# Left-operand sums of a seven-product output projection: accumulating transfers in the place of VectorE's additions

## The chip, the core and the metric

One NeuronCore of a Trainium2 chip runs the whole program in one launch. The metric is device time in microseconds (us), as the median over executions; a profile of one execution stands beside it.

## What is computed

One layer of an encoder block over 1024 tokens of width 1024: a feed-forward half step, a mixer (neighbourhood attention and a state-space branch, merged by gates), a second feed-forward half step, an embedding of the input, a norm. The change lies in the mixer's merge and its output projection:

```
g_attn, g_ssm = jnp.split(jax.nn.sigmoid(gates), N_BRANCH, axis=-1)
h = h + (g_attn * y_attn + g_ssm * y_ssm) @ w_out[i]
h = h + 0.5 * swiglu(rms_norm(h, ffn2_norm[i]), ...)
```

All arithmetic is float32. A product is made of three matmuls: each operand is split into a rounded part (hi, by a ScalarE copy into the reduced type, line 151) and the rest (lo, by a VectorE subtraction, line 152), and hi x hi, hi x lo and lo x hi are summed (`mm3`, lines 182 to 184).

## The kernel before, in words

Activations lie transposed, channels on the 128 partitions, tokens along the free dimension in two halves t = 0, 1 of 512. A tile is 128 x 512 float32, 256 KB.

The merge makes sixteen tiles `mg[m, t]` (m = 0 to 7 are the channel blocks): `branches` multiplies the two mixer outputs by their weights, `gated` (lines 1501 and 1502) multiplies by the gates and adds.

The output projection is a product of 2 x 2 blocks by seven block products instead of eight (`A7` gives their left operands: a12, a11, s1, s2, s4, s3, a22). For each block index j = 0 to 3 the left operand's four blocks are a = mg[j, 0], b = mg[4+j, 0], c = mg[j, 1], d = mg[4+j, 1]. The seven left operands are b, a, the first sum s1 = c + d, the second sum s2 = s1 - a, the third sum s4 = b - s2, the difference s3 = a - c, and d. `out_left` returns the operand of product i and the additions that follow its split: line 1519 makes s1 (`ss`) behind product 1, lines 1522 and 1523 make s2 and s3 behind product 2, line 1526 makes s4 behind product 3. All sixteen (four lines, four j) run on VectorE.

The right operands, blocks of the weight w_out, need sums too. They are made by `taken_from` (lines 406 and 407): ScalarE turns the sign of the block and a transfer issued from GpSimd (`G.dma_start` with `accum_op=add`) adds the other block from HBM onto it.

There are 28 steps (i, j), product i outermost. `out_prep` (split of the left operand, right operand by `b_operand`, then the additions) runs four steps (LA) ahead of `out_run`, which issues twelve matmuls onto four banks. The products go to banks dz, dx, dy (ACC7 = Z X Y X Y X X); at j = 3 line 1548 adds the four banks onto the residual h on VectorE, and for i = 1, 4, 5, 6 `merged` adds the squares for the next norm (ScalarE line 221 or 224, VectorE line 225) and stores h. At step 20 the next norm's statistic for t = 0 is started: a matmul by a matrix of ones over the summed squares (line 241), then lines 203 to 206, and the scaling of h by line 372 with its splits.

TensorE's instructions keep the order in which they are written. Those of the other engines and the GpSimd transfers are put in order by a planner at build time, which simulates the engines and goes by priority; line 1548 and `gated` have a raised priority. On the chip each engine's queue then runs in that fixed order, and each instruction waits for its own operands and buffers. Buffers that matter: `w` (20 tiles, the weight splits; the next stage takes twelve of them from step 4 on), `tmp` (17 tiles, the left splits ah and al, gates, squares), `hid` (the pool of 56 tiles with mg, ss and the weight blocks).

Of the kernel before, what the change touches and what calls it, by code (L numbers as in the profile page):

```python
# [8 lines left out]
F32 = mybir.dt.float32  # L9
F32R = mybir.dt.float32r  # L10
I32 = mybir.dt.int32
AF = mybir.ActivationFunctionType
ALU = mybir.AluOpType
# [25 lines left out]
def encoder_block(ctx, tc, I, out):  # L39
    nc = tc.nc  # L40
    V, A, G, T = nc.vector, nc.scalar, nc.gpsimd, nc.tensor
# [26 lines left out]
    def at(kind, shape, dt, name):  # L68
        pool, tag, bufs = cur[kind]
        return pool.tile(list(shape), dt, tag=tag, bufs=bufs, name=name)  # L70
# [7 lines left out]
    def thid(name, shape=(P, HT), dt=F32R):  # L78
        return at("hid", shape, dt, name)

    def tmp(name, shape=(P, HT), dt=F32):
        return at("tmp", shape, dt, name)
# [67 lines left out]
    def split(hi, lo, src, eng=V):  # L150
        A.copy(hi, src)  # L151
        return eng.tensor_tensor(lo, src, hi.bitcast(F32), ALU.subtract)  # L152
# [16 lines left out]
    def loadh(src, st_kind="tmp", w_kind="w", eng=V):  # L169

        res = []
        for i in range(2):
            st = at(st_kind, [P, HT], F32, "wsh")
            nc.sync.dma_start(st, src[:, i * HT:(i + 1) * HT])
            hi, lo = at(w_kind, [P, HT], F32R, "whh"), at(w_kind, [P, HT], F32R, "whl")
            split(hi, lo, st, eng)
            res += [(hi[:, ksl(k)], lo[:, ksl(k)]) for k in range(4)]
        return res
# [230 lines left out]
    def b_operand(blk, i, src=None):  # L409


        b11, b12, b21, b22 = blk
        if src is None and i in (2, 3, 6):
            V.tensor_tensor(b11, (b12, b22, None, None, b21)[i - 2], b11, ALU.subtract)  # L414
        elif src is None and i == 5:
            V.tensor_tensor(b12, b22, b12, ALU.subtract)
        hi, lo = tw("wh", [P, HT]), tw("wl", [P, HT])
        mark["ins"] = split(hi, lo, (b21, b11, b11, b11, b22, b12, b11)[i]).ins
        if src is not None and i in (1, 2, 3):
            taken_from(blk, 0, src[(1, 3, 2)[i - 1]])  # L420
            if i == 2:
                taken_from(blk, 1, src[3])
        return hi, lo
# [1055 lines left out]
    def branches(W, todo):  # L1479

        for i, t, b in todo:
            o = banks[i, t, b] = bank("br")
            for k in range(4):
                mm3(o, W[i][4 * b + k], oy[t][b][k], k == 0, k == 3)
                tick()

    def gates(m, t):
        gts = []
        for b in range(2):
            gt = tmp("gt")  # L1490
            nc.sync.dma_start(gt, g_d[8 * b + m, :, hsl(t)])
            A.activation(gt, gt, AF.Sigmoid)
            gts.append(gt)
        return gts

    def gated(gts, m, i, t):

        mg[m, t] = thid("mg", dt=F32)
        with tc.high_priority(offset=PRI):
            for b, gt in enumerate(gts):  # L1500
                V.tensor_tensor(gt, banks.pop((i, t, b)), gt, ALU.mult)
            V.tensor_tensor(mg[m, t], gts[0], gts[1], ALU.add)

    def out_place(n, j):

        return I["wout"][j + (n // 2) * 4][:, (n % 2) * HT:(n % 2 + 1) * HT]

    def out_load(n):
        for j in range(4):
            blk[j][n] = at("hid", [P, HT], F32, "wblk")  # L1510
            nc.sync.dma_start(blk[j][n], out_place(n, j))

    def out_left(i, j):

        a, b, c, d = (mg.get((m, t)) for t in range(2) for m in (j, 4 + j))

        def s1():
            ss[j] = thid("ss", dt=F32)
            V.tensor_tensor(ss[j], c, d, ALU.add)

        def s2():
            V.tensor_tensor(ss[j], ss[j], a, ALU.subtract)
            V.tensor_tensor(c, a, c, ALU.subtract)

        def s4():
            V.tensor_tensor(b, b, ss[j], ALU.subtract)

        return (b, a, ss.get(j), ss.get(j), b, c, d)[i], {1: s1, 2: s2, 3: s4}.get(i)

    def out_prep(i, j):  # L1530
        src, then = out_left(i, j)
        left = tmp("ah", dt=F32R), tmp("al", dt=F32R)
        split(*left, src)
        made[i, j] = left, b_operand(blk[j], i, [out_place(n, j) for n in range(4)])
        if then is not None:
            then()
# [15 lines left out]
    banks, Wn, mg, ss, made, acc = {}, W0, {}, {}, {}, {}  # L1552
# [3 lines left out]
    for m0 in range(0, NK, 2):  # L1556
        W, Wn = Wn, []
        if m0 == 0:
            Wn = [loadh(I["was"][2 + i]) for i in range(2)]

            branches(W, [(i, t, 0) for t in range(2) for i in range(2)])
        for t in range(2):
            for i in range(2):
                if t == 1 and 0 < m0 < NK - 2:
                    Wn.append(loadh(I["was"][m0 + 2 + i]))
                gts = gates(m0 + i, t)
                branches(W, [(i, t, b) for b in range(m0 == 0, 2)])
                gated(gts, m0 + i, i, t)
            if m0 == NK - 2 and t == 0:
                for s_ in steps[:LA]:  # L1570
                    out_prep(*s_)
        if m0 in (2, 4):
            out_load(2 if m0 == 2 else 0)
    for n in (1, 3):
        out_load(n)
    for n_, (i, j) in enumerate(steps):
        if n_ == 4:
            s7 = Seven(h, 2)
            ffn = Ffn(s7, I["wg2"], I["wu2"], I["wd2"], a2_d, load_h2, done, t0_done2, (8, 11))
            for n in (0, 2, 1, 3):  # L1580
                ffn.load_first(n)
        if n_ == 12:
            for g in range(2):
                ffn.prep(("C", "11", g))
        if n_ == 20:
            start(s7.first(4, 5, 2))
        if n_ + LA < len(steps):
            out_prep(*steps[n_ + LA])
        out_run(i, j)
# [196 lines left out]
def build(nc, shapes):  # L1786
    ins = {k: nc.dram_tensor("in_" + k, s, F32, kind="ExternalInput").ap() for k, s in shapes.items()}
    out = nc.dram_tensor("outT", (1024, SEQ), F32, kind="ExternalOutput").ap()
    with tile.TileContext(nc, schedule_with_timeline_sim=True) as tc:
        with tc.manual_schedule(engines={mybir.EngineType.PE}):  # L1790
            encoder_block(tc, ins, out)
# [12 lines left out]
```

## Time and profile before

| | |
|---|---|
| median of three runs | 2105.99 us (2104.8 to 2106.98) |
| the profiled execution's own time | 2106.49 us |
| its span, first to last instruction | 2104.7 us |
| granted TensorE clock, mean | 0.996 |
| TensorE busy | 2077.2 us (99%) |
| VectorE / ScalarE / GpSimd busy | 1414.2 / 1000.3 / 401.7 us |
| the merge's output projection, steps 0 to 27 | about 1259 to 1346 us of the span |

The page names engines PE (TensorE matmuls), PEld (its weight loads), DVE (VectorE), ACT (ScalarE), POOL (GpSimd), SP (SyncE's queue); a q behind the name is that engine's queue. Times run from the span's start. A line such as L152 is the line of the kernel, and as `split` is a helper, one line stands for splits all over the kernel; the tile names tell them apart (al <- ss is the left operand's split, wl <- wblk the weight's).

### The profile page before, as it was taken

The numbers are of one execution on the slowest core, as the hardware profiler recorded it, in microseconds if no ns is written. First come the engines' busy times: TensorE is split into PE (matmuls) and PEld (weight loads), VectorE is DVE, ScalarE is ACT, GpSimd is POOL, SyncE is SP. The second block draws the span as 40 slices with busy tenths as digits, with TensorE's granted clock in tenths as the row PEclk, the third lists the DMA queues.
The fourth block names the chain that finished last, engine by engine and source line by source line (L and its number), as shares of the span: only waits on it lengthen the run. The fifth ranks groups of instructions, "written<-read, shape, count | busy, mean of one in ns | idle before, by whom it ended". The sixth has DMA issues, their size and how long they took to land.

```text
span 2104.7 us, 28050 instructions
## 1 busy us (share of the span) xinstructions
PE 2077.2 (99%) x9660; PEld 1707.4 (81%) x9660; DVE 1414.2 (67%) x2420; ACT 1000.3 (48%) x1832; POOL 401.7 (19%) x636
## 2 busy tenths in 40 slices
PE   8999999999999999999999999899999999999997
PEld 3788888888888888888888888788888888888886
DVE  7897776667967334777653658896566665786855
ACT  6434333434445333667674635543333334445544
POOL 0047555541000006888100011000000000000000
PEclk9999999999999999999999999999999999999999
DMA  3434444475533552233477754143323338533302
GB/s 133 143 118 154 126 134 126 140 269 165 185 119 107 167 177 68 64 102 97 120 202 263 254 171 91 56 159 111 110 85 126 90 112 296 158 109 92 119 21 81
DMA packets 197455, 285.19 MB, mean 136 GB/s; under 512 B 41536, under 2 KB 80576, under 8 KB 197312
## 3 DMA queue, kind: packets, MB, share of 16 engines
q1 hardware_dynamic: 180160, 258.22, 38.9%
q10 hardware_dynamic: 14848, 20.98, 2.9%
q0 software_dynamic: 2304, 4.20, 1.3%
q8 instruction: 76, 1.25, 0.3%
q14 instruction: 67, 0.55, 0.1%
HBM read 201.01 MB, written 82.31 MB: 135 GB/s over the span
## 4 chain that ended last, share of the span: by engine, by line
PE 93%; DVE 4%; ACT 1%; DMA 1%; issue 1%; SPq 0%; DVEq 0%; ACTq 0%
PE dx L182 4%; PE dx L183 4%; PE dx L184 4%; PE ux L182 3%; PE ux L184 3%; PE ux L183 3%; PE gx L182 3%; PE gx L183 3%; PE gx L184 3%; PE gt L182 3%; PE gt L183 3%; PE gt L184 3%; PE dy L183 2%; PE dy L182 2%; PE dy L184 2%; PE uy L182 2%
## 5 line engine op out<-in xcount | busy, mean ns | idle before, releaser
L151 ACT CAST wh<-hbuf 128x512 fp32r<-128x512 f32 x280 | 172.9, 622 | 392.3 <-PE gx L183 84.0
L152 DVE TENSOR_TENSOR wl<-hbuf,wh 128x512 fp32r<-128x512 f32 x280 | 210.4, 754 | 125.2 <-ACT wh L151 123.0
L151 ACT CAST wh<-wblk 128x512 fp32r<-128x512 f32 x190 | 117.8, 622 | 182.5 <-PE dx L183 78.5
L182 PE MATMUL dx<-ah,wh 128*128 128x512 f32 x416 | 164.0, 394 | 3.9 <-DVE hbuf L1548 3.6
L152 DVE TENSOR_TENSOR wl<-wblk,wh 128x512 fp32r<-128x512 f32 x190 | 130.3, 688 | 53.4 <-ACT wh L151 48.0
L184 PE MATMUL dx<-ah,wl 128*128 128x512 f32 x416 | 162.3, 390 | 0.0
L183 PE MATMUL dx<-al,wh 128*128 128x512 f32 x416 | 162.3, 390 | 0.0
L152 DVE TENSOR_TENSOR al<-araw,ah 128x512 fp32r<-128x512 f32 x154 | 106.0, 692 | 53.7 <-PE dx L183 21.1
L1086 POOL TENSOR_TENSOR sc<-X,rho 128x128 f32<-128x128 f32 x128 | 77.9, 609 | 327.1 <-ACT X L1069 317.1
L182 PE MATMUL gx<-xh,wh 128*128 128x512 f32 x320 | 125.0, 391 | 1.3 <-DVE c L571 1.2
L182 PE MATMUL ux<-xh,wh 128*128 128x512 f32 x320 | 125.1, 391 | 0.3 <-DVE c L571 0.3
L184 PE MATMUL gx<-xh,wl 128*128 128x512 f32 x320 | 124.5, 389 | 0.0
L184 PE MATMUL ux<-xh,wl 128*128 128x512 f32 x320 | 124.5, 389 | 0.0
L183 PE MATMUL ux<-xl,wh 128*128 128x512 f32 x320 | 124.5, 389 | 0.0
L183 PE MATMUL gx<-xl,wh 128*128 128x512 f32 x320 | 124.5, 389 | 0.0
L151 ACT CAST ah<-araw 128x512 fp32r<-128x512 f32 x154 | 95.0, 619 | 47.5 <-PE dx L183 12.7
L182 PE MATMUL gt<-xh,wh 128*128 128x512 f32 x256 | 103.0, 402 | 0.0
L183 PE MATMUL gt<-xl,wh 128*128 128x512 f32 x256 | 99.9, 390 | 0.0
L184 PE MATMUL gt<-xh,wl 128*128 128x512 f32 x256 | 99.8, 390 | 0.0
L182 PEld LDWEIGHTS dx<-ah,wh 128*128 128x128 f32 x416 | 78.4, 188 | 21.8 <-issue 4.7
L414 DVE TENSOR_TENSOR hbuf<-hbuf 128x512 f32<-128x512 f32 x120 | 91.2, 761 | 2.1
L183 PEld LDWEIGHTS dx<-al,wh 128*128 128x128 f32 x416 | 78.5, 189 | 16.8 <-issue 0.7
(379 smaller groups left out, 5592.0 us busy)
## 6 DMA issues: line engine op xcount, KB each, us to landing
araw<-a_d SPq DMA_DIRECT2D x154, 256.0 KB
a_d<-c SPq DMA_DIRECT2D x148, 256.0 KB
wblk<-in_wd SPq DMA_DIRECT2D x88, 256.0 KB
hbuf<-in_wg SPq DMA_DIRECT2D x40, 512.0 KB
hbuf<-in_wu SPq DMA_DIRECT2D x40, 512.0 KB
wst<-in_win SPq DMA_DIRECT2D x26, 512.0 KB
hbuf<-in_xT SPq DMA_DIRECT2D x32, 256.0 KB
h_d<-hbuf ACTq DMA_DIRECT2D x32, 256.0 KB
```

Source lines behind the costliest of these rows:

```text
L151: A.copy(hi, src)
L152: return eng.tensor_tensor(lo, src, hi.bitcast(F32), ALU.subtract)
L182: T.matmul(o, lhsT=wh, rhs=xh, start=first, stop=False, skip_group_check=more)
L183: T.matmul(o, lhsT=wh, rhs=xl, start=False, stop=False, skip_group_check=more)
L184: T.matmul(o, lhsT=wl, rhs=xh, start=False, stop=last, skip_group_check=more)
L414: V.tensor_tensor(b11, (b12, b22, None, None, b21)[i - 2], b11, ALU.subtract)
L1086: G.tensor_tensor(sc, both, rho4, ALU.mult)
```

## The change

The first sum starts as a ScalarE copy of c, and a transfer from GpSimd accumulates d onto it (`out_sum`); this is placed ahead: for j = 0, 1 behind the first half of the last pair of blocks, for j = 2, 3 behind the second. Behind the split of a (product 1), ScalarE turns the sign of a in place. Behind the split of s1 (product 2), two transfers accumulate the turned a onto ss (s2) and onto c, which becomes c - a. Behind the split of s2 (product 3), ScalarE turns ss and a transfer accumulates b onto it (s4 = b - s2). The left operand of product 4 is now ss, and that of product 5 is -c: its split takes the turned sign into the ScalarE copy and into a scalar_tensor_tensor on VectorE.

```
+    def plus(dst, src):
+        G.dma_start(dst, src, accum_op=ALU.add)
+    def out_sum(j):
+        ss[j] = thid("ss", dt=F32)
+        A.copy(ss[j], mg[j, 1])
+        plus(ss[j], mg[4 + j, 1])
     def out_left(i, j):
         a, b, c, d = (mg.get((m, t)) for t in range(2) for m in (j, 4 + j))
-        def s1():
-            ss[j] = thid("ss", dt=F32)
-            V.tensor_tensor(ss[j], c, d, ALU.add)
+        def turn(x):
+            A.activation(x, x, AF.Copy, scale=-1.0)
         def s2():
-            V.tensor_tensor(ss[j], ss[j], a, ALU.subtract)
-            V.tensor_tensor(c, a, c, ALU.subtract)
+            plus(ss[j], a)
+            plus(c, a)
         def s4():
-            V.tensor_tensor(b, b, ss[j], ALU.subtract)
-        return (b, a, ss.get(j), ss.get(j), b, c, d)[i], {1: s1, 2: s2, 3: s4}.get(i)
+            turn(ss[j])
+            plus(ss[j], b)
+        return (b, a, ss.get(j), ss.get(j), ss.get(j), c, d)[i], {1: lambda: turn(a), 2: s2, 3: s4}.get(i)
     def out_prep(i, j):
         src, then = out_left(i, j)
-        left = tmp("ah", dt=F32R), tmp("al", dt=F32R)
-        split(*left, src)
+        hi, lo = left = tmp("ah", dt=F32R), tmp("al", dt=F32R)
+        if i == 5:
+            A.activation(hi, src, AF.Copy, scale=-1.0)
+            V.scalar_tensor_tensor(lo, src, -1.0, hi.bitcast(F32), ALU.mult, ALU.subtract)
+        else:
+            split(hi, lo, src)
...
             if m0 == NK - 2 and t == 0:
+                for j in range(2):
+                    out_sum(j)
                 for s_ in steps[:LA]:
                     out_prep(*s_)
...
+    for j in range(2, 4):
+        out_sum(j)
     for n in (1, 3):
         out_load(n)
```

## Rows read from the trace of the kernel before

**Rows 1.** From the page: busy time, share of the span and instructions of each engine; and the chain of work that ended last, by engine.
```profile
PE 2077.2 (99%) x9660; PEld 1707.4 (81%) x9660; DVE 1414.2 (67%) x2420; ACT 1000.3 (48%) x1832; POOL 401.7 (19%) x636
...
PE 93%; DVE 4%; ACT 1%; DMA 1%; issue 1%; SPq 0%; DVEq 0%; ACTq 0%
```

**Rows 2.** The waits of TensorE over the whole span: who waited for whom, us in total, times, the longest.
```profile
PE dx L182 <- DVE hbuf L1548: 3.6, 1, 3.6
PE ms L241 <- DVE acc L225: 3.4, 2, 2.6
```

**Rows 3.** Busy time of each engine by stretch: start and end, length, busy us (instructions) of PE, PEld, DVE, ACT and POOL, then granted TensorE clock, mean busy share of the DMA engines, GB/s.
```profile
1260.00:1300.00 40.00, 40.00 (x178) 33.14 (x177) 38.80 (x65) 25.91 (x47) 10.49 (x12) 1.00 0.61 111
1300.00:1312.00 12.00, 12.00 (x54) 9.93 (x54) 6.67 (x11) 3.64 (x6) 0.00 (x0) 1.00 0.00 1
1312.00:1320.00 8.00, 5.39 (x24) 3.90 (x22) 6.99 (x12) 5.26 (x8) 0.00 (x0) 1.00 0.35 131
1320.00:1342.00 22.00, 18.42 (x75) 14.73 (x74) 19.96 (x32) 10.95 (x19) 0.00 (x0) 0.92 0.13 48
```

**Rows 4.** VectorE's instructions in order of time up to the first wait of TensorE: start, us, line and operation, tiles, and in brackets the idle time before it with its releaser.
```profile
1306.12 0.69 DVE L152 TENSOR_TENSOR wl<-wblk,wh 128x512 fp32r<-128x512 f32 x1 [0.80 <-ACT wh L151]
...
1311.61 0.69 DVE L152 TENSOR_TENSOR wl<-wblk,wh 128x512 fp32r<-128x512 f32 x1 [2.07 <-ACT wh L151]
1312.21 1.88 DVE L1548 TENSOR_TENSOR hbuf<-hbuf,dy 128x512 f32<-128x512 f32 x3
...
1315.21 0.68 DVE L152 TENSOR_TENSOR wl<-wblk,wh 128x512 fp32r<-128x512 f32 x1
...
1317.21 0.68 DVE L152 TENSOR_TENSOR al<-mg,ah 128x512 fp32r<-128x512 f32 x1
1317.81 0.68 DVE L152 TENSOR_TENSOR wl<-wblk,wh 128x512 fp32r<-128x512 f32 x1
1318.41 0.68 DVE L225 TENSOR_TENSOR acc<-acc,sq 128x512 f32<-128x512 f32 x1
```

**Rows 5.** ScalarE's groups of instructions from 1290 to 1312: busy us, mean ns of one, and the idle time before them with what ended it.
```profile
L151 ACT CAST wh<-wblk 128x512 fp32r<-128x512 f32 x8 | 5.0, 621 | 10.5 <-PE dy L183 6.3 <-PE dx L183 4.2
```

**Rows 6.** VectorE's groups from 1320 to 1342 (as in rows 5), then the line 1548 instruction of that stretch in order of time.
```profile
L372 DVE SCALAR_TENSOR_TENSOR hbuf<-hbuf,gains,rs 128x512 f32<-128x512 f32 x8 | 5.8, 745 | 0.0
L152 DVE TENSOR_TENSOR xl<-hbuf,xh 128x512 fp32r<-128x512 f32 x8 | 5.4, 682 | 0.0
...
1331.21 0.68 DVE L1548 TENSOR_TENSOR hbuf<-hbuf,dx 128x512 f32<-128x512 f32 x1
```

**Rows 7.** TensorE's matmuls behind its second wait, in order of time (columns as in rows 4).
```profile
1332.04 0.76 PE L182 MATMUL dx<-ah,wh 128*128 128x512 f32 x1 [3.58 <-DVE hbuf L1548]
1332.60 0.63 PE L183 MATMUL dx<-al,wh 128*128 128x512 f32 x1
1333.03 0.63 PE L184 MATMUL dx<-ah,wl 128*128 128x512 f32 x1
```

**Rows 8.** VectorE's groups from 1260 to 1300: the four lines of the sums.
```profile
L1526 DVE TENSOR_TENSOR mg<-mg,ss 128x512 f32<-128x512 f32 x4 | 2.6, 681 | 0.0
L1522 DVE TENSOR_TENSOR ss<-ss,mg 128x512 f32<-128x512 f32 x4 | 2.6, 681 | 0.0
L1523 DVE TENSOR_TENSOR mg<-mg 128x512 f32<-128x512 f32 x4 | 2.6, 681 | 0.0
...
L1519 DVE TENSOR_TENSOR ss<-mg 128x512 f32<-128x512 f32 x4 | 2.5, 684 | 0.0
```

**Rows 9.** The instructions of lines 406 and 407 over the span: duration in ns (least / median / most), first and last start, form; and for the transfers of line 407 the time from issue to landing.
```profile
L406 ACT ACTIVATE wblk<-wblk x16: 616/630/635, 1241.7 to 1284.2; 128x512 f32<-128x512 f32 x16
...
L407 POOL DMA_DIRECT2D wblk<-in_wout x16: 856/864/1774, 1242.7 to 1285.2; - x16
...
DMA to landing us min/median/max: 4.0/6.2/9.4
```

**Rows 10.** VectorE in order of time (columns as in rows 4): the last merged tile, the first and last split of the first sum, the first and the last two of the second sum.
```profile
1260.66 0.68 DVE L1502 TENSOR_TENSOR mg<-gt 128x512 f32<-128x512 f32 x1
...
1266.83 0.68 DVE L152 TENSOR_TENSOR al<-ss,ah 128x512 fp32r<-128x512 f32 x1
...
1273.44 0.68 DVE L152 TENSOR_TENSOR al<-ss,ah 128x512 fp32r<-128x512 f32 x1
...
1286.66 0.68 DVE L152 TENSOR_TENSOR al<-ss,ah 128x512 fp32r<-128x512 f32 x1
...
1289.07 1.28 DVE L152 TENSOR_TENSOR al<-ss,ah 128x512 fp32r<-128x512 f32 x2
```

**Rows 11.** TensorE in order of time: the first matmul of products 2, 3 and 4.
```profile
1281.01 0.39 PE L182 MATMUL dy<-ah,wh 128*128 128x512 f32 x1
...
1291.89 0.39 PE L182 MATMUL dx<-ah,wh 128*128 128x512 f32 x1
...
1302.77 0.39 PE L182 MATMUL dy<-ah,wh 128*128 128x512 f32 x1
```

**Rows 12.** The DMA queues from 1240 to 1300: packets, MB, and the time of their packets as a share of 16 engines' 60 us. GpSimd's transfers are the software queue.
```profile
q0 software_dynamic: 2304, 4.20, 44.1%
```

**Rows 13.** Busy time by stretch, columns as in rows 3.
```profile
1260.00:1290.00 30.00, 30.00 (x134) 24.86 (x133) 29.43 (x50) 20.64 (x38) 10.49 (x12) 1.00 0.81 148
1290.00:1302.00 12.00, 12.00 (x55) 9.93 (x54) 10.93 (x19) 6.43 (x12) 0.00 (x0) 1.00 0.01 2
```

## The prediction

> **What bounds the kernel now.** Start with the page's busy line and its chain of work: TensorE is busy for 99% of the span and carries 93% of the chain that ended last [rows 1]. A change to VectorE can therefore pay only where TensorE is seen to wait. Next, the waits of TensorE over the span: two matter here, 3.6 us in front of a matmul onto bank dx, released by VectorE's line 1548, and 3.4 us (2.6 of it in one wait) in front of the norm's sum, released by VectorE's line 225 [rows 2]. Third, the busy time by stretch. From 1260 to 1300 us, where the merge's output projection is prepared and begun, VectorE is busy 38.8 of 40 us, and yet TensorE is busy 40 of 40. From 1300 to 1312 VectorE drops to 6.67 of 12, TensorE is still full. Only from 1312 to 1342 does TensorE lose time: 8 - 5.39 = 2.6 us and 22 - 18.42 = 3.6 us [rows 3]. So the congested stretch of VectorE and the stretch in which TensorE waits are two different ones, with slack in between. That is the reading on which the forecast rests.
>
> Why there is slack in between: before its splits of 1306 and 1311.6 us VectorE stands idle 0.8 and 2.07 us, waiting for ScalarE's cast of a weight block [rows 4]. ScalarE in turn waits for TensorE: of its idle time from 1290 to 1312, 10.5 us is in front of those casts and ended by matmuls dy and dx [rows 5], which must give back a weight tile first. VectorE has thus caught up by 1306 and runs at TensorE's cadence. The first stall comes after that: from 1312.21 VectorE works without a gap through four line 1548 additions, the squares' sums and two splits until 1319.1 us [rows 4], and the norm's matmul waits for the last of these. The second: line 1548 for the next bank is placed at 1331.21, among the norm's eight scalings and eight splits of that stretch [rows 6], and TensorE waits 3.58 us, resumes at 1332.04 and first runs seven matmuls at the lower of its clock's two levels: they start 0.43 us apart [rows 7] instead of the 0.227 that follow from 48 matmuls between 1281.01 and 1291.89 [rows 11]; the granted clock of the stretch is 0.92 [rows 3].
>
> **What is removed.** Lines 1519, 1522, 1523 and 1526, four instructions each: 2.5 + 2.6 + 2.6 + 2.6 = 10.3 us of VectorE, all between 1263 and 1281 [rows 8]. TensorE did not wait for them there. Their removal lets VectorE catch up earlier than 1304 and wait longer for weight tiles; the work after 1312 is the same work, released by the same matmuls. Gain on the path: 0. It would be more only if the instruction order of 1312 to 1332 changed, which is a rival below.
>
> **What is added on ScalarE.** Four copies of mg into ss and eight sign turns, 12 x 0.63 us = 7.6 us by the row of the same kind of activation, line 406 [rows 9]. From 1260 to 1300 ScalarE is busy 25.9 of 40 [rows 3], so 33.5 of 40 after: hidden behind TensorE, whose steps are prepared four ahead (4 x 2.72 us). If that cover were gone, each 0.63 us would delay a cast, and the cast a step. The last left operands' step (i = 5) turns its sign inside its split: VectorE uses a scalar_tensor_tensor in place of the subtraction, 0.74 instead of 0.68 us [rows 6], 4 x 0.06 = 0.24 us in the stretch where VectorE idles: 0.
>
> **What is added on GpSimd's queue.** Sixteen accumulating transfers of 256 KB from tile to tile. The nearest rows are the sixteen accumulating transfers of weights from HBM, line 407: 0.86 us of issue each, and 4.0 to 9.4 us from issue to landing, median 6.2 [rows 9]. A source in SBUF is not shown in this trace; I take the same range, both ends kept, since kind, size and destination are the same. Twelve of the sixteen old issues lie in 1260 to 1300; GpSimd goes from 10.5 to about 10.5 + 14 x 0.86 = 22.5 us of 40 there [rows 3]. It does nothing else then, and its queued weight transfers would be later by a few issues.
>
> Then each sum against the matmul that needs it, at the slowest landing seen (9.4) plus the issue (0.86):
> - First sum (ss = c + d): the last mg is written at 1260.66 + 0.68 = 1261.3 [rows 10]; landed by 1271.6. It is needed by the fourth step of dy, 1281.0 + 3 x 2.72 = 1289.2 [rows 11], less 1.3 for the split: 16 us to spare.
> - Second sum (ss - a) for j = 0: the split that must be over ends at 1266.83 + 0.68 [rows 10]; landed by 1277.8, 12.8 us ahead of the split that step i = 3 needs (its matmul starts at 1291.9 [rows 11]). For j = 3 it ends at 1273.44 + 0.68 = 1274.1; even behind the eight issues of this step (6.9 us) it lands by 1290.4, 8 us ahead of its matmul at 1291.9 + 8.2 less the split.
> - Third sum (b - ss) for j = 0, the tight one: the split of ss ends at 1286.66 + 0.68 = 1287.3 [rows 10]; turn 0.63, issue 0.86, landing 9.4: 1298.2; split 0.62 + 0.68: 1299.5. The matmul that takes it starts at 1302.77 [rows 11]. 3.3 us to spare at the slowest landing, 6.5 at the median. For j = 3 the splits of ss are over at 1289.07 + 1.28 = 1290.4 and its matmul comes three steps later: 8 us.
> - The sums for step i = 5 are made with the second sum and needed 22 us later.
>
> So every added latency is covered, and the sum is 0 on the path. The profiled execution took 2106.49 us (span 2104.7 and 1.8 around it), 0.5 us above the median 2105.99 of the three runs; against that median the forecast is 2106.0, and a difference under 0.2% (4.2 us) is what a measurement of this kernel can hardly tell from none.
>
> The landing time can be taken otherwise. The Trainium skill, "DMA: Bandwidth & Descriptors", section "Anatomy of one DMA", fits a transfer issued from GpSimd as 2.0 us plus bytes over 436 GB/s. For 256 KB that is an estimate of 2.6 us, under the fastest landing of this trace. By it the third sum would have 10 us to spare and the first rival below could not occur; the rows of accumulating transfers disagree with it, and they decide.
>
> **Rivals.**
> 1. *Slower: the transfers queue up and the third sum comes late.* The DMA engines are the resource already taken: the sixteen accumulating transfers hold 44.1% of all engines over 60 us, 1.65 us each [rows 12], and from 1260 to 1290 the engines are busy 0.81 [rows 13], which leaves 5.7 us. Ten of the added transfers (two first sums, eight of the second step) bring 16.5 us into that stretch: 10.8 us spill past 1290, where the engines were idle. Queued behind them, the first third-sum transfer starts at 1300.8 and lands its 4.0 us later, 1304.8; split, 1306.1. TensorE would wait 1306.1 - 1302.8 = 3.3 us at the first dy matmul of i = 4, and seven matmuls at the lower clock add 7 x 0.2 = 1.4 [rows 7]: 4.7 us, 2110.7. With 9.4 instead of 4.0 it is 10.1 us, 2116.1. The later three come 1.65 us apart against steps of 2.72 and add nothing. It decides from the point where the landing exceeds 9.4 + 3.3 = 12.7 us. For it: engines at 0.81, and ScalarE's and VectorE's queues are in order, so a split placed too early would hold the weight casts behind it. Against it: transfers from tile to tile need not read HBM, two of the first sums can run before 1260, and the engines are at 0.01 from 1290 to 1302 [rows 13]. Chance 0.25.
> 2. *Faster: the order on VectorE changes where TensorE waits.* The order of VectorE's and ScalarE's instructions is planned, and a planner with ten microseconds less on VectorE may put the line 225 sums and line 1548 ahead of the splits of 1315 to 1331. Without the three splits in between [rows 4] the first stall loses 3 x 0.6 = 1.8 us, without the second, 3.6 + 1.4: together 6.8 us, 2099.2. Against it: the relief ends at 1304 while these instructions depend on matmuls from 1312 on. Chance 0.12.
> 3. *The forecast*, both stalls as they are: 0.63, within 2104 to 2109 as the stalls move by an instruction or two.
>
> **How the numbers follow.** Of rival 1's 0.25 nearly all lies above 2110.2, say 0.23; of rival 2's 0.12, 0.11 below 2101.8; the rest, 0.66, is within 0.2%. The range takes in the forecast's own 2104 to 2109, the lower half of rival 1 (to 2112.5) and the edge of rival 2 (from 2101.5); about 0.1 is left out above and 0.08 below.
>
> **What would show it.** In the profile after: VectorE's busy time from 1260 to 1300 near 29 of 40 and no wait of TensorE from 1260 to 1312; the two waits of [rows 2] again, 2.6 and 3.6 us; accumulating transfers x32 in the software queue with landings of 4 to 10 us. A wait of TensorE at the first dy matmul of i = 4, released by VectorE's split of ss or by ScalarE waiting for a transfer into ss, would show the forecast wrong and rival 1 right; a missing wait at the norm's sum or at dx would show rival 2.

## The result and the profile after

The changed kernel takes 2109.65 us (median of 17 runs, 2107.65 to 2112.39) against 2106.13 us of the kernel before in the same comparison (17 runs): ratio 1.0016, 95% interval 1.0009 to 1.0023. That is 3.5 us slower: under the 0.2% that the forecast took as its bound, but the interval excludes no change. The profiled execution took 2109.32 us, its span 2107.6.

The page's busy line and the chain by engine, as in [rows 1]:
```profile
PE 2077.0 (99%) x9660; PEld 1706.6 (81%) x9660; DVE 1404.8 (67%) x2404; ACT 1005.7 (48%) x1844; POOL 415.7 (20%) x652
...
PE 91%; DVE 5%; ACT 1%; DMA 1%; issue 1%; SPq 0%; DVEq 0%; ACTq 0%
```
TensorE has the same work. VectorE has 9.4 us less of it, and still its share of the chain of work that ended last went from 4% to 5%: TensorE waits for it longer. The waits of TensorE over the span, to set beside [rows 2]:
```profile
PE ms L241 <- DVE acc L225: 7.2, 3, 6.3
...
PE dx L182 <- DVE hbuf L1563: 2.0, 2, 1.9
```
The wait for the norm's squares grew from 2.6 to 6.3 us, the one at dx (line 1548 is line 1563 now) fell from 3.6 to 1.9. The stretches of [rows 3]:
```profile
1260.00:1300.00 40.00, 40.00 (x178) 33.14 (x177) 24.97 (x41) 25.38 (x47) 21.00 (x24) 1.00 1.07 217
1300.00:1312.00 12.00, 12.00 (x54) 9.93 (x54) 8.68 (x15) 6.97 (x13) 0.00 (x0) 1.00 0.25 45
1312.00:1320.00 8.00, 3.18 (x15) 2.29 (x13) 7.90 (x14) 4.54 (x8) 0.00 (x0) 1.00 0.35 131
1320.00:1342.00 22.00, 18.51 (x66) 13.82 (x67) 19.08 (x32) 11.55 (x20) 0.00 (x0) 0.84 0.13 48
```
From 1260 to 1300 VectorE fell from 38.8 to 25.0 us, by 3.5 more than the removed 10.3, while from 1300 to 1312 it rose from 6.67 to 8.68 and ScalarE from 3.64 to 6.97. Work has slid out of the stretch where VectorE has room. The last but one column points to a reason: the mean busy share of the DMA engines, 0.61 before, is 1.07.

Why the work slid is read from the transfers first, the new ones (line 1515) and the old ones (line 407): duration of the issue in ns, first and last start, and the time from issue to landing.
```profile
L1515 POOL DMA_DIRECT2D ss<-mg x12: 861/876/2135, 1244.7 to 1298.4; - x12
L1515 POOL DMA_DIRECT2D mg<-mg x4: 854/875/1220, 1255.1 to 1268.0; - x4
...
DMA to landing us min/median/max: 5.0/8.3/11.7
```
```profile
L407 POOL DMA_DIRECT2D wblk<-in_wout x16: 858/867/1837, 1241.3 to 1295.8; - x16
...
DMA to landing us min/median/max: 4.1/9.5/11.8
```
The old transfers' median landing went from 6.2 to 9.5 us: they pay for the new ones too. GpSimd's issues in order of time, then the landing of the two transfers issued at 1278.58 and 1279.84:
```profile
1267.98 0.87 POOL L1515 DMA_DIRECT2D mg<-mg  x1 [0.97 <-DMA ss<-mg]
...
1278.58 0.89 POOL L1515 DMA_DIRECT2D ss<-mg  x1 [0.26 <-DVE hbuf L1563]
...
1296.36 1.21 POOL L1515 DMA_DIRECT2D ss<-mg  x1
```
```profile
DMA to landing us min/median/max: 11.4/11.5/11.6
```
Slow landings hold back the issues too. From 1267.98 to 1282.46 eleven issues in a row leave 0.2 to 0.4 us after the landing of the transfer issued seven before them: that of 1278.58 behind the one of 1267.98, which took 10.3 us and landed at 1278.3. ScalarE's instructions in order of time, with the idle time and its releaser in brackets:
```profile
1290.11 0.62 ACT L151 CAST ah<-ss 128x512 fp32r<-128x512 f32 x1 [1.43 <-PE dy L184]
...
1291.16 2.69 ACT L151 CAST wh<-wblk 128x512 fp32r<-128x512 f32 x5
...
1295.33 0.61 ACT L1529 ACTIVATE ss<-ss 128x512 f32<-128x512 f32 x1
...
1303.57 0.62 ACT L151 CAST ah<-ss 128x512 fp32r<-128x512 f32 x1 [4.51 <-DMA ss<-mg]
...
1308.52 2.17 ACT L151 CAST wh<-wblk 128x512 fp32r<-128x512 f32 x4
```
Here the lateness can be followed. The split of the first sum of j = 2 ended on VectorE at 1269.6. The transfer that makes the second sum from it was issued 9.0 us later, at 1278.6, and took 11.4 us to land, at 1290.0; the second sum's split starts then, at 1290.11 (the row names a matmul as what ended the wait; in the repetition of the change below the same instruction has the same 1.43 us put down to the transfer). The sign turn for the third sum could run from 1291.5, but stands at 1295.33, behind five weight casts, two sign turns of weights and the split of j = 3. Its transfer leaves at 1296.36, and its split can start at 1303.57. Until then ScalarE stands idle for 4.51 us, with everything else behind in its queue: the last split of product 4, the four splits of product 5 and the weight casts. On VectorE, then, the same stretch as in [rows 4]:
```profile
1304.23 0.69 DVE L152 TENSOR_TENSOR al<-ss,ah 128x512 fp32r<-128x512 f32 x1 [3.32 <-ACT ah L151]
...
1309.12 1.87 DVE L1563 TENSOR_TENSOR hbuf<-hbuf,dx 128x512 f32<-128x512 f32 x3
...
1312.12 2.49 DVE L152 TENSOR_TENSOR wl<-wblk,wh 128x512 fp32r<-128x512 f32 x4
1314.53 1.87 DVE L1563 TENSOR_TENSOR hbuf<-hbuf,dy 128x512 f32<-128x512 f32 x3
...
1320.72 0.68 DVE L225 TENSOR_TENSOR acc<-acc,sq 128x512 f32<-128x512 f32 x1
```
From 1304.23 on VectorE works without a gap: the splits that it did at TensorE's cadence before, idle in between, now come in one block, and the first line 1563 addition on dy is the piece that waits behind the block. VectorE's own queue adds to it. The four additions on dx, which ran from 1301.65 on before, could have filled most of the 3.32 us that VectorE stood idle, as the last matmul onto dx starts at 1301.19; but they stand behind the late split and start at 1309.12. TensorE, to be read with [rows 7] and [rows 11]:
```profile
1301.42 0.39 PE L182 MATMUL dy<-ah,wh 128*128 128x512 f32 x1
...
1321.46 2.07 PE L241 MATMUL ms<-acc,ones 128*128 128x512 f32 x2 [6.28 <-DVE acc L225]
1322.54 1.42 PE L182 MATMUL dx<-ah,wh 128*128 128x512 f32 x1
1323.76 0.63 PE L183 MATMUL dx<-al,wh 128*128 128x512 f32 x1
...
1335.30 0.47 PE L182 MATMUL dx<-ah,wh 128*128 128x512 f32 x1 [1.86 <-DVE hbuf L1563]
```
The balance is taken from the first dy matmul of product 4, where this execution was 1.35 us ahead of that of before. (That difference comes from earlier stretches and was not followed; over the profiled executions of all kernels here this matmul starts between 1299.1 and 1303.1.) To the first addition on dy it is 1314.53 - 1301.42 = 13.11 us, before 1312.21 - 1302.77 = 9.44 [rows 4, 11]: **3.67 us later**. The norm's matmul then starts at the clock's lower level and takes 2.07 us, before 1.12: 0.95 more, and the matmuls behind it start 0.43 us apart at first. At dx the wait is 1.86 us, and the slow matmuls of [rows 7] do not come again: from the first addition on dx to the last product's first addition it is 1344.88 - 1334.47 = 10.41 us, before 1342.55 - 1331.21 = 11.34 [rows 6], so 0.93 comes back. The rows are from the change, the last one from before:
```profile
1334.47 0.68 DVE L1563 TENSOR_TENSOR hbuf<-hbuf,dx 128x512 f32<-128x512 f32 x1
...
1344.88 2.05 DVE L1563 TENSOR_TENSOR hbuf<-hbuf,dx 128x512 f32<-128x512 f32 x3 [0.59 <-PE dx L184]
```
```profile
1342.55 2.05 DVE L1548 TENSOR_TENSOR hbuf<-hbuf,dx 128x512 f32<-128x512 f32 x3 [1.52 <-PE dx L184]
```
From 1301.42 to 1344.88 it is 43.46 us, before 39.78: 3.68 us more, near the 3.5 between the medians. (With the 1.35 us of head start 2.3 of them show at this place, and the two profiled spans differ by 2.9.)

### The profile page after: what moved, and what is told of

Same layout as the page of the kernel before. It is cut to its first block, busy times and chain, and to the rows that moved or that the text cites. A ratio compares the mean times of both kernels' runs of the same rounds, so it can differ in the third digit from the quotient of the medians.

```text
span 2107.6 us, 28087 instructions
## 1 busy us (share of the span) xinstructions
PE 2077.0 (99%) x9660; PEld 1706.6 (81%) x9660; DVE 1404.8 (67%) x2404; ACT 1005.7 (48%) x1844; POOL 415.7 (20%) x652
## 4 chain that ended last, share of the span: by engine, by line
PE 91%; DVE 5%; ACT 1%; DMA 1%; issue 1%; SPq 0%; DVEq 0%; ACTq 0%
PE dx L182 4%; PE dx L183 4%; PE dx L184 4%; PE gx L182 3%; PE ux L182 3%; PE gx L183 3%; PE ux L183 3%; PE ux L184 3%; PE gx L184 3%; PE gt L182 3%; PE gt L183 2%; PE gt L184 2%; PE dy L184 2%; PE dy L182 2%; PE dy L183 2%; PE uy L182 2%
## 5 line engine op out<-in xcount | busy, mean ns | idle before, releaser
L151 ACT CAST ah<-araw 128x512 fp32r<-128x512 f32 x154 | 94.9, 619 | 42.7 <-PE dx L183 12.7
```

## Experiments

Theory 1: the new transfers fill the DMA engines, the two-hop chain (second sum, split, turn, third sum) then lands late, ScalarE's queue stands in front of it, VectorE comes late to the squares, and TensorE pays at the norm's matmul. Theory 2: the twelve added ScalarE instructions make the loss by themselves. Theory 3: the chain is too long by itself, on idle DMA engines too.

**The change once more**, as it is, beside later runs:

> The change itself once more, beside the same runs of the kernel before as the two runs with it: ratio 1.0009 to 1.0023 as in its first measurement, the norm's wait near 6 us and ScalarE standing over 3 us for a third sum. A ratio under 1.0006 would mean that the runs with parts undone showed the spread between chips and not the parts.

2108.55 against 2105.13 us, ratio 1.0017 (1.0009 to 1.0026).
```profile
PE ms L241 <- DVE acc L225: 6.0, 3, 5.1
```
```profile
1288.57 0.62 ACT L151 CAST ah<-ss 128x512 fp32r<-128x512 f32 x1 [1.43 <-DMA ss<-mg]
...
1301.17 0.62 ACT L151 CAST ah<-ss 128x512 fp32r<-128x512 f32 x1 [3.63 <-DMA ss<-mg]
```
The wait at the norm was 5.1 us, ScalarE's for a third sum 3.6, and the first addition on dy came 11.9 us after the first dy matmul, 2.5 later than before. The norm's matmul took 2.07 us again, and at dx the slow matmuls came as before, so nothing was given back: to the last product's first addition it is 43.2 us, 3.4 more than before. The loss is the change's, and it is made up a little differently in each execution.

**ScalarE's work alone**, in the kernel before:
```
+        def same(x):
+            A.activation(x, x, AF.Copy, scale=1.0)
         def s1():
...
             V.tensor_tensor(ss[j], c, d, ALU.add)
+            same(ss[j])
+            same(a)
...
         def s4():
+            same(ss[j])
             V.tensor_tensor(b, b, ss[j], ALU.subtract)
```


> The kernel before with twelve more ScalarE activations of 128x512 at the places of the change's copies and sign turns (copies of a tile onto itself by factor 1.0), and no new transfer; VectorE keeps its additions. Theory 1: no change, ratio 0.9997 to 1.0005, TensorE's waits 2.6 and 3.6 us as before. Theory 2: ratio about 1.0016, with the norm's wait near 6 us. Theory 3: no change.

Ratio 1.0002 (0.9994 to 1.0011); 2104.99 us. The waits of TensorE:
```profile
PE ms L241 <- DVE acc L225: 3.4, 2, 2.6
PE dx L182 <- DVE hbuf L1554: 2.6, 2, 2.4
```
The norm's wait is unchanged with twelve more activations, and the one at dx has not grown (2.4 us). Theory 2 falls.

**A quarter of the bytes**: the changed kernel, with three quarters of every sum left out:
```
-        G.dma_start(dst, src, accum_op=ALU.add)
+        G.dma_start(dst[:, 0:P], src[:, 0:P], accum_op=ALU.add)
```


> The changed kernel with every one of its sixteen new transfers cut to a quarter of the columns (128 of 512); the other three quarters of the left operands' sums are left out. Waits, ScalarE work, instruction counts and issues stay. Theory 1 (the new transfers fill the DMA engines from 1250 to 1300 us, share 1.07 in the profile after; landings grow to 8 to 12 us and ScalarE's queue stands in front of late sums, so VectorE reaches the norm's squares late): landings back to about 4 to 8 us, no wait of ScalarE for ss over 1 us, the norm's wait on TensorE back to about 2.6 us, time within 1 us of the kernel before (ratio 1.0000 to 1.0005). Theory 2 (the twelve added ScalarE instructions are what delays the casts): as slow as the change, ratio 1.0016. Theory 3 (the chain turn, issue, landing is too long by itself, even on idle DMA engines): between, 1.0008 to 1.0016, with ScalarE still waiting for the third sums.

Ratio 1.0001 (0.9992 to 1.0010). The instructions, what each of them waits for and the issues are those of the change, and the loss is gone. The order that the planner wrote is not: on ScalarE three instructions stand between the split of the second sum of j = 2 and its sign turn, nine in the change. So this run does not part the engines' load from the order. TensorE's waits, and ScalarE's waits for sums (1255 to 1320):
```profile
PE dx L182 <- DVE hbuf L1563: 3.6, 1, 3.6
PE ms L241 <- DVE acc L225: 3.5, 3, 2.6
```
```profile
ACT ah L151 <- DMA ss<-mg: 4.3, 2, 3.1
```
One detail of the expectation missed: ScalarE still stood 3.1 us for a third sum, but at 1295.9, not 1303.6, so that it had caught up before dy ended. A wait of ScalarE is no loss by itself; what counts is when it ends.

**The third sum back on VectorE**, the other twelve transfers kept:
```
         def s4():
-            turn(ss[j])
-            plus(ss[j], b)
+            V.tensor_tensor(b, b, ss[j], ALU.subtract)
...
```


> The changed kernel with the third sum (b - ss) back as a VectorE subtraction; first sum, second sum and difference stay transfers (28 accumulating transfers instead of 32, eight of the twelve new ScalarE instructions). Theory 1: the DMA engines stay full until about 1290, but no left operand waits for a landing after 1292, so ScalarE's 4.5 us wait goes and the norm's wait is back near 3 us: ratio 1.0000 to 1.0006. Theory 2: two thirds of the loss stay, 1.0011. Theory 3: 1.0000.

Ratio 1.0001 (0.9993 to 1.0010). The engines stay at 0.99 from 1260 to 1300 and the new transfers still land in 6.6 to 11.6 us, but no split waits for them after 1290. Up to there ScalarE's instructions come in the change's order, less the turns; its last two waits for weight blocks are 3.06 and 1.38 us (3.15 and 0.85 in the change), and the split of the second sum of j = 2 waits for its landing as long (1.44 us, 1.43 in the change). That row, and TensorE's waits:
```profile
1289.82 0.62 ACT L151 CAST ah<-ss 128x512 fp32r<-128x512 f32 x1 [1.44 <-DMA ss<-mg]
```
```profile
PE ms L241 <- DVE acc L225: 3.9, 2, 3.1
...
PE dx L182 <- DVE hbuf L1562: 2.2, 2, 2.0
```
The first addition on dy is 9.9 us behind the first dy matmul (13.1 in the change, 9.4 before). Full engines, late weight blocks and a late second sum without the second hop cost 0.5 us at this place, and nothing that the interval shows.

**Load without a reader**: the kernel before, with sixteen accumulating transfers from the merged tiles into scratch in HBM:
```
+        def more(k):
+            G.dma_start(f_d[4 * j + k], d, accum_op=ALU.add)
         def s1():
+            more(0)
...
         def s2():
+            more(1)
+            more(2)
...
         def s4():
+            more(3)
...
```


> The kernel before, its VectorE additions kept, with sixteen more accumulating transfers of 256 KB from the merged tiles into scratch in HBM that nothing reads: load on GpSimd's queue and on the DMA engines without anyone waiting for the new transfers; only the sixteen old weight transfers can come late. Theory 1: landings grow to 8 us and more, ScalarE waits some us for weight blocks, but these have 10 us and more of slack, so at most a third of the loss: ratio 1.0000 to 1.0006. A variant of theory 1, in which the late weight blocks and not the left sums make the loss: 1.0010 to 1.0020, with ScalarE waiting for weight blocks and the norm's wait near 5 to 6 us. Theory 2: no change.

Ratio 0.9996 (0.9987 to 1.0005). Waits of ScalarE from 1255 to 1320, and the landings of the weight transfers:
```profile
ACT wh L151 <- DMA wblk<-in_wout: 8.2, 5, 3.4
```
```profile
DMA to landing us min/median/max: 3.9/9.7/14.2
```
The weight blocks come as late as in the change or later, ScalarE waits 8.2 us for them, and the norm's wait stays 2.6 us. The unread transfers leave from 1231 to 1267, earlier than the change's, and the engines are at 0.88 from 1260 to 1300, so this is not the change's load over again; but the variant of theory 1 in which late weight blocks alone make the loss finds no support here, nor in the run above.

**The third sum alone by transfer**, in the kernel before:
```
         def s4():
-            V.tensor_tensor(b, b, ss[j], ALU.subtract)
+            A.activation(ss[j], ss[j], AF.Copy, scale=-1.0)
+            G.dma_start(ss[j], b, accum_op=ALU.add)
...
```


> The kernel before with only the third sum made the new way: ScalarE turns the sign of ss, a transfer accumulates b onto it (four new full-size transfers, 20 in all); first sum, second sum and difference stay on VectorE. Theory 1 (contention: the third sum is late because the DMA engines are full and the second sums before it land late): its landings 4 to 6 us on engines idle after 1290, no ScalarE wait over 1.5 us, the norm's wait 2.6 us, ratio 0.9996 to 1.0005. Theory 3 (the hop turn, issue, landing is too long by itself): ScalarE waits 2 to 5 us for ss between 1290 and 1304, the norm's wait 4 to 6 us, ratio 1.0008 to 1.0016.

Ratio 0.9996 (0.9987 to 1.0005). The landings of the four new transfers, and what ScalarE waits for them (1255 to 1320):
```profile
L1527 POOL DMA_DIRECT2D ss<-mg x4: 862/867/1152, 1286.2 to 1289.0; - x4
...
DMA to landing us min/median/max: 3.3/4.0/4.9
```
```profile
ACT ah L151 <- DMA ss<-mg: 2.4, 4, 0.9
```
The same hop on emptier engines (0.71 from 1260 to 1300) lands in 3.3 to 4.9 us instead of 5.0 to 7.8, the last leaves at 1289.0 instead of 1298.4, and it costs nothing.

**Both hops, eight transfers fewer**: first sum and difference on VectorE, second and third sums by transfer.
```
-        A.copy(ss[j], mg[j, 1])
-        plus(ss[j], mg[4 + j, 1])
+        V.tensor_tensor(ss[j], mg[j, 1], mg[4 + j, 1], ALU.add)
...
-            plus(c, a)
+            V.tensor_tensor(c, c, a, ALU.add)
```


> The changed kernel with the first sum and the difference c - a on VectorE, the second and third sums by transfers as changed (24 accumulating transfers instead of 32; the chain of two hops per j stays). Theory 1: the engines' share from 1260 to 1300 falls to about 0.85, the second sums land in 6 to 9 us instead of 9 to 12, the third sums are ready some 3 us earlier: ratio 1.0000 to 1.0007, norm's wait 2.6 to 3.5 us. Theory 3: as slow as the change, 1.0012 to 1.0018, since both hops are kept.

Ratio 0.9996 (0.9988 to 1.0005); the engines at 0.84, the new landings:
```profile
L1515 POOL DMA_DIRECT2D ss<-mg x8: 861/867/2442, 1263.1 to 1290.5; - x8
...
DMA to landing us min/median/max: 3.3/4.2/8.8
```
The norm's wait is 2.6 us. Theory 3 falls: the whole chain fits when the engines are less full (in an order that the planner wrote anew here too).

One measure separates the change from all these runs. From the first dy matmul of product 4 to the first addition on dy it is 9.4 us before and in every run above without the loss, but for 9.9 with the third sum back on VectorE; it is 11.9 and 13.1 in the two executions of the change. To the last product's first addition it is 39.8 us before, 39.8 to 40.9 in those runs, and 43.2 and 43.5 in the change.

**Where TensorE pays.** The norm's matmul is started twelve matmul groups later, with the scalings one group behind it instead of five, in the kernel before and in the changed one:
```
-            start(s7.first(4, 5, 2))
+            start(s7.first(16, 1, 2))
```


> The kernel before with the norm's matmul for the first half of the tokens issued sixteen matmul groups (one product, 10.9 us) into product 5 and 6 instead of four (2.7 us), and its scalings one group after: TensorE meets the finished sum instead of waiting for it, and line 1548 of product 5 comes free of the scalings. Expected: both waits of TensorE (2.6 and 3.6 us) gone or under 1 us each; as a version of its own, ratio 0.9965 to 0.9985 (4 to 7 us), unless the next stage's first operands come late instead (then a new wait at its first matmul, ratio 0.999 to 1.001).

> The changed kernel with the same later norm matmul as in e7_stat16. Theory 1, with the loss entering TensorE only at the norm's wait: VectorE's lateness of 2 to 3 us at the squares is covered by the 8.2 us of matmuls put in between, so this run is within 0.0005 of e7_stat16. If the lateness reaches TensorE elsewhere too (at line 1563 of later products, or at the next stage's operands), it stays 1 to 3 us slower than e7_stat16.

Before with it: 2101.23 us, 0.9980 (0.9971 to 0.9988). The change with it: 2102.20 us, 0.9985 (0.9976 to 0.9993), both against the same runs of the kernel before. The two are 1.0 us apart (their intervals overlap) where the unaltered pair is 3.5 apart, with the DMA engines of the second still at 1.08 and ScalarE still waiting 8.7 us in all for sums. TensorE's waits in the changed kernel with the later matmul:
```profile
PE g L183 <- DVE xl L152: 2.6, 3, 1.5
...
PE ms L241 <- DVE acc L225: 0.8, 1, 0.8
```
The 0.8 us is another norm's wait, elsewhere in the span; of the one here nothing is left, though the first addition on dy still comes 11.4 us after the first dy matmul. So the lateness reaches TensorE at the norm's wait and, with that moved, hardly anywhere else.

**A version that beats both.** Both runs change the kernel before. The first has the scalings one group behind the norm's matmul and one in every two groups, the second four groups behind and one per group:
```
-            start(s7.first(4, 5, 2))
+            start(s7.first(12, 1, 2))        # e11_stat12
+            start(s7.first(12, 4, 1))        # e12_stat12_late
```


> The kernel before with the norm's matmul twelve matmul groups into product 5 (four before, sixteen in e7_stat16) and its scalings one group after. If what costs is only that TensorE must not meet an unfinished sum, both old waits go and the next stage's first operands come 2.7 us earlier than in e7_stat16, so its new wait of 2.4 us there goes too: ratio 0.9965 to 0.9978. If the scalings then stand before line 1548 of product 5 again, the wait at dx comes back in part: 0.998 to 0.999.

> As e11_stat12, but with the scalings four groups behind the norm's matmul and one per group, so that line 1548 of product 5 is planned ahead of them: the wait at dx goes; the next stage's first operands are at most as late as in e7_stat16: ratio 0.9965 to 0.998.

2100.55 us, 0.9977 (0.9968 to 0.9986), and 2100.24 us, 0.9977 (0.9967 to 0.9987): 4.6 and 4.9 us faster than the kernel before, 8 us faster than the change beside them. The last one's waits of TensorE from 1300 to 1360:
```profile
PE g L183 <- DVE xl L152: 1.5, 3, 0.9
PE dx L182 <- DVE hbuf L1548: 0.3, 1, 0.3
```
Both old waits are gone but for 0.3 us at dx, and with them the slow matmuls (granted clock 1.00 from 1312 to 1342, 0.94 before). What remains is 1.5 us at the next stage's first operands.

## Why the prediction came out as it did

- **Where TensorE waits: right.** It is busy 40 of 40 and 12 of 12 us up to 1312 in both kernels, and its two waits are those of [rows 2].
- **The removed additions are worth nothing: right.** VectorE's 10.3 us went and no wait of TensorE in their stretch with them; the version at the end keeps all of them and beats both kernels.
- **ScalarE's twelve instructions cost nothing: right**, by the run with ScalarE's work alone (1.0002).
- **The landing times: too short.** 4.0 to 9.4 us were taken over from the rows of before [rows 9]; the new ones took 5.0 to 11.7. The spill that rival 1 worked out from [rows 12, 13] did happen, with the engines at 1.07 from 1260 to 1300 and 0.25 from 1300 to 1312. For the second sum of j = 3 the prediction allowed 6.9 us in GpSimd's queue, and it took 6.4 (1273.46 to 1279.84); j = 2, which it left out, took 9.0, as issues waited for earlier landings. The old weight transfers' median went from 6.2 to 9.5 us. The Trainium skill, "DMA: Bandwidth & Descriptors", section "Issuing engines are not separate DMA queues", says that transfers of all issuers run on the same 16 engines and interleave. Here both kinds are issued from GpSimd, so the 6.2 and 9.5 us agree with it for one issuer, and no run here shows it across issuers.
- **The third sum: the step that failed.** "So every added latency is covered, and the sum is 0 on the path" set each sum against the matmul that takes it, and only for j = 0 and j = 3. That test still passes after the change: TensorE does not wait at dy, and the tightest sum, j = 2, is split by 1304.9, 1.9 us ahead of its matmul at 1301.42 + 2 x 2.72 = 1306.9. But the instruction that waits for the transfer stands in ScalarE's queue, and what is behind it there has a deadline too. ScalarE stood until 1303.57, VectorE's block of splits and additions on dx then reached 1314.5, and the additions on dy and squares behind it were 3.67 us late where VectorE had been taken to be idle. The term was 0 in the sum and measures 3.7 in the change's profile and 3.4 in its repetition.
- **Rival 1 had the cause and the wrong place.** Full engines and in-order queues were named in it; TensorE was to wait at the first dy matmul (3.3 us and 1.4 of low clock). It waited at the norm instead, 3.7 us longer (6.3 against 2.6). The rival was to begin with a landing over 12.7 us; the loss came with none over 11.8. The matmuls at the lower clock came at the norm in place of dx in the change, at both in its repetition.
- **Rival 2 did not happen.** The order on VectorE from the additions on dy to those on dx is that of before, piece by piece.
- **The number.** 2106.0 was forecast, 2109.65 measured, within 2101.5 to 2112.5; no change over 0.2% was the likeliest case and holds, but the narrower 2104 to 2109 given for it does not. That the time lies in the range is owed to the part of it that was there for rival 1, not to the working of the forecast, whose own signs failed: VectorE was busy 25.0 us from 1260 to 1300 and not 29, the two waits are 6.3 and 1.9 us and not 2.6 and 3.6, and landings reach 11.8 us and not 10. Its sign for 1260 to 1312, no wait of TensorE, came true. And the 0.2% that a measurement could hardly tell from none was too wide: 17 runs of each told 0.16% from none.

What stays open is how much of the relief in the runs with parts undone comes from the freer DMA engines and how much from the other order that the planner then writes. The runs with a quarter of the bytes, with the third sum alone and with eight transfers fewer have freer engines and another order at once. The run with the third sum back on VectorE keeps the load and, up to 1290, ScalarE's order; it shows that the second hop is needed for the loss. No run keeps the change's order on freer engines. Where between 28 and 32 transfers the loss begins was not tried, nor were the weight loads of the next stage, which run in the same stretch, moved away.

## What to carry to other kernels

Set an added latency not only against the consumer of the data, but against every instruction that queues behind the one that waits: the deadline is that of the most urgent one behind it. Before moving work from a compute engine onto transfers, read the DMA engines' share in that stretch and add the new transfers to it: two hops in a row were free at a share of 0.84 and late at 1.07 (in two different orders of instructions). And where TensorE waits twice for the same engine, moving the instruction that waits a few groups later may be worth more (here 4.6 to 4.9 us) than lightening the engine (here nothing).

## What the runs showed of the hardware

- An accumulating transfer of 256 KB from tile to tile landed 3.3 to 4.9 us after its issue with the DMA engines at a busy share of 0.71 (the third sum alone by transfer), and 5.0 to 11.7 us beside fifteen others and sixteen from HBM, with the engines at 1.07. Cut to a quarter of the columns it still took 2.4 us at the least; by estimate from 2.4 and 3.3, most of the quiet time is not the bytes.
- In the change GpSimd had at most seven transfers under way from 1267.98 to 1282.46: each issue there left 0.2 to 0.4 us after the landing of the one seven before it. What sets this number was not looked into.
- Beside sixteen unread transfers of that kind the weight transfers landed in up to 14.2 us (9.4 before), and the time did not move (0.9996).
- After a wait of 2.6 us the norm's matmul pair took 1.12 us in the kernel before and in the run with a quarter of the bytes, but 2.05 and 2.08 us in the runs with unread transfers and with eight transfers fewer; in the change it took 2.07 behind 6.3 us. So the length of the wait alone does not tell here whether the clock falls to its lower level.
